# Two-layer decoder trunk in fp32: norm gains folded into weights, pauses in background weight splitting, and earlier gate weights in layer 0

## The chip, the cores and the metric

The kernel runs on one core of one Trainium2 chip. The metric is the device time of one execution in microseconds (us). The engines are PE (TensorE: matmuls and transposes; PEld is its weight load), DVE (VectorE), ACT (ScalarE), POOL (GpSimd) and SP, whose queue issues every DMA of this kernel. Each engine works through its own instructions strictly in order; an instruction whose input is late holds all that stand behind it on that engine.

## The reference

Two layers on 1024 tokens of width 1024. Layer 0 is gated linear attention (GLA) with 4 heads, layer 1 a sparse attention with an indexer and top-k. Each mixer is followed by a residual, a layer norm and a gated embedding.

```python
def layer_norm(x, g, b):
    mu = jnp.mean(x, axis=-1, keepdims=True)
    var = jnp.mean(jnp.square(x - mu), axis=-1, keepdims=True)
    return (x - mu) * lax.rsqrt(var + NORM_EPS) * g + b

# GLA, after the chunked attention has given o per head (512 wide):
    o = o * lax.rsqrt(jnp.mean(o * o, axis=-1, keepdims=True) + NORM_EPS)
    o = o.reshape(B, L, D_INNER) * gn_g
    return (o * jax.nn.silu(z)) @ w_out

# every layer:
    x = layer_norm(ALPHA * x + y, ln_g[i], ln_b[i])          # ALPHA = 4 ** 0.25
    x = x + (p[i] @ ple_w[i]) * jax.nn.sigmoid(x @ ple_gate_w[i])
```

## The kernel before

Every fp32 product is made of three matmuls: each operand is split into a high part (rounded, by ACT) and a low part (the rest, a subtraction by DVE), and hi x hi, hi x lo and lo x hi are summed. All tiles are 128 x 512 or so.

Layer 0 works on two halves of 512 tokens. In each half it runs over the 4 heads. For a head it computes v, the gate, q and k (`v_phase`, `g_phase`, `qk_phase`); then four chunks of 128 tokens run through the steps s1 to s4 of `core_steps`, spread between the matmuls of the output projection of the head before (`out_phase`) and of z for the next head (`z_phase`). The first head of a half has only z to run beside, so its four chunks are packed into about half the time of the others.

The order of the instructions is written by a recorder, `Flow`. It keeps a clock (`fl.now`) that advances with each recorded matmul, and a heap of steps with due times. The order on every engine comes from these due times and not from the chip. Two background streams are paced by the same clock:

- `Weights` (`W`) loads the weights of layer 0 (`wst`, 512 KB each) and splits them into `whi` (ACT, L173) and `wlo` (DVE, L175) shortly before use.
- `split_ahead`, driven by `bg3`, does the same for the weights that layer 1 and the index projections need. Each of 130 half tiles is loaded into `pst` (L200), split on ACT into `phi` (L209) and on DVE in place (L213), and both parts are stored to DRAM (`whs` L211, `wls` L215). One step is due every 2.15 us of the recorder's clock, three steps a piece.

In the second half the top-k counts of the index scores (`tkj`, `tki`, L1032 and L1082 to L1085) run on DVE beside this.

Names that matter below:

- `y` is the residual sum of a half, 128 x 4 x 1024. `load_y` loads the tokens' x into it (2048 KB) and scales it by ALPHA on POOL (L1185). The memory serves as staging for x in feature order before (`y<-in_x_T`).
- `wa2f` are the weights of the second gate projection of one head, loaded by `g_load` in three small DMAs (L459) and split into `w` by `g_split` (ACT L464, DVE L385).
- `o` is a chunk's output in PSUM, `ot` its copy by DVE (L700), `junk` the ACT pass that sums its squares (L702), `oT` the transpose on PE, `uf` its product with z (DVE L725), `u` the two split parts of that.
- `z` is silu of the gate path (ACT L597), times `gn`, the gain of the group norm, on POOL (L593).
- `tr`, `kh`, `kl`, `Af`, `Ah`, `Al`, `S`, `R` are a chunk's scores and transposed keys, their split parts, and the running state; `m` and `ta` are k and q times their decays.
- `ix`, `rl` and `sc` are the index scores of the first half: PE, relu on ACT (L1014), sum on DVE (L1008, L1010). `zz` at L976 is the value projection's copy. They run while the second half starts (`start_half(1)`, which loads the next x and the first `wst`).

Of the kernel before, what the change touches and what calls it, by code (L numbers as in the profile page):

```python
# [10 lines left out]
F32 = mybir.dt.float32  # L11
# [5 lines left out]
AF = mybir.ActivationFunctionType  # L17
# [30 lines left out]
class Flow:  # L48


    def __init__(self, nc):
        self.pe = nc.tensor
        self.now, self.n, self.heap, self.pacers = 0.0, 0, [], []
# [18 lines left out]
    def chain(self, *steps):  # L72

        (_, first), rest = steps[0], steps[1:]
        first()
        if rest:
            self.after(rest[0][0], lambda: self.chain((0, rest[0][1]), *rest[1:]))
# [60 lines left out]
class Weights:  # L138

    def __init__(self, nc, pool, seq, dram, after):
        self.nc, self.pool, self.seq, self.dram, self.after = nc, pool, seq, dram, after
        self.nd = self.ns = self.nu = self.part = 0
        self.due = 0.0
        self.staged, self.parts, self.ahead = {}, {}, {}

    def pace(self, now):
        if now >= self.due and self.step():
# [2 lines left out]
    def step(self):  # L152
        n, i = self.ns, self.part
        if n == len(self.seq):
            return False
        whole = n not in self.staged and self.seq[n][0] in self.ahead
        if n >= self.nu + (3 if whole and self.seq[self.nu - 1][0][0] != "do" else 2):
            return False
        if i == 0:
            if not whole:  # L160
                self.loads(n + 1)
            self.parts[n] = tuple(self.pool.tile([128, 1024], F32R, tag=t, name=t, bufs=4) for t in ("whi", "wlo"))
        if whole:
            for part, there in zip(self.parts[n], self.ahead[self.seq[n][0]]):
                self.nc.sync.dma_start(part.bitcast(F32), there)
            self.ns += 1
            self.loads(min(self.ns + 1, self.nu + 3))
            return True
        st = self.staged[n]
        hi, lo = self.parts[n]  # L170
        c = slice((i % 2) * 512, (i % 2) * 512 + 512)
        if i < 2:
            self.nc.scalar.activation(hi[:, c], st[:, c], AF.Copy)  # L173
        else:
            self.nc.vector.tensor_sub(lo[:, c], st[:, c], hi[:, c].bitcast(F32))  # L175
        self.part = (i + 1) % 4
        if i == 3:
            self.staged.pop(n)
            self.ns += 1
            self.after(1.5, lambda: self.loads(self.ns + 2))  # L180
        return True
# [73 lines left out]
def trunk_kernel(ctx, tc, x_tok, x_T, p_T, pos, freq, g_q, g_k, g_v, g_z, g_a, g_a2, g_ba, g_gn, g_o,  # L255
# [98 lines left out]
    kflip = cp.tile([128, 8], F32, name="kflip")  # L354
    pool.iota(kflip, pattern=[[128, 8]], base=-254, channel_multiplier=1, allow_small_or_imprecise_dtypes=True)
    ba = cp.tile([128, 8], F32, name="ba")
    gn = cp.tile([128, 16], F32, name="gn")
    lngb = cp.tile([128, 2, 2, 8], F32, name="lngb")
    fq = cp.tile([128, 4], F32, name="fq")
    Afs = []  # L360
# [96 lines left out]
    def g_load(h):  # L457
        for i in range(3):
            nc.sync.dma_start(wa2f[32 * i:32 * i + 16, :], g_a2[:, h * 256:(h + 1) * 256])  # L459
# [127 lines left out]
    def z_phase(u, X):  # L587
        h = u["h"]
        zt = lp.tile([128, 4, HT], F32, tag="z", name="z", bufs=2)
        for b in range(4):  # L590
            def ev(ps, b=b):
                def scale():
                    pool.tensor_scalar(zt[:, b], zt[:, b], gn[:, 4 * h + b:4 * h + b + 1], 0.0,  # L593
                                       op0=OP.mult, op1=OP.add)
                    if b == 3:
                        u["z"] = zt
                chain((0, lambda: act.activation(zt[:, b], ps, AF.Silu)), (0.8, scale))  # L597

            yield from fm_block(("z", 4 * h + b), X, ev)

    def core_steps(u):
# [107 lines left out]
        def s4(c):  # L709
            def f():  # L710
                cs = slice(c * 128, c * 128 + 128)
                fl.req(("o", c) in st, "z" in u, h == 0 or u["prev"].get("out", 0) > c)
                ot = st.pop(("o", c))
                ps = pp.tile([128, 4, 128], F32, tag="oT", name="oT")
                for b in range(4):
                    fl.transpose(ps[:, b], ot[:, b * 128:b * 128 + 128], ident)
                uf = lp.tile([128, 4, 128], F32, tag="uf", name="uf", bufs=2)
                uh, ul = t2k("u", F32R), t2k("u", F32R)

                def done():  # L720
                    rc = slice(c, c + 1)
                    pool.tensor_scalar(u["rs"][:, rc], u["ss"][:, rc], 1.0 / 512.0, EPS, op0=OP.mult, op1=OP.add)
                    pool.tensor_tensor(u["rs"][:, rc], u["rs"][:, rc], mhalf[:, rc], op=OP.pow)
                    u["u"][c] = uh, ul
                chain((0, lambda: dve.tensor_mul(uf, ps, u["z"][:, :, cs])),  # L725
                      (0.8, lambda: split(uh, ul, uf.rearrange("p b t -> p (b t)"), done)))
            return f
# [50 lines left out]
            P.append((ph, pl))  # L778
        return P

    def norm_steps(y, np_):

        st8 = np_.tile([128, 4, 2, 6], F32, tag="bn", name="bn")
        mv = np_.tile([128, 4, 2], F32, tag="mv", name="mv")
        rstd = np_.tile([128, 4], F32, tag="rstd", name="rstd")
        f_done = [False] * 4

        def norm(t):
            def power():
                pool.tensor_scalar(rstd[:, t:t + 1], mv[:, t, 1:2], EPS, 1.0, op0=OP.add, op1=OP.mult)  # L790
                pool.tensor_tensor(rstd[:, t:t + 1], rstd[:, t:t + 1], mhalf[:, :1], op=OP.pow)

            def stats():
                for c in range(2):
                    dve.bn_stats(st8[:, t, c], y[:, t, c * 512:c * 512 + 512])  # L795
                dve.bn_aggr(mv[:, t], st8[:, t])
                power()

            def apply():
                dve.tensor_scalar(y[:, t], y[:, t], mv[:, t, 0:1], rstd[:, t:t + 1],  # L800
                                  op0=OP.subtract, op1=OP.mult)
                f_done[t] = True
            chain((0, stats), (2.0, apply))
        return norm, f_done
# [365 lines left out]
    for half in range(NH):  # L1170
# [9 lines left out]
        y = X.y  # L1180

        def load_y(y=y, half=half):
            nc.sync.dma_start(y, x_tok[half * HT:(half + 1) * HT, :].rearrange("(t p) d -> p t d", p=128))
            for t in range(4):
                pool.tensor_scalar(y[:, t], y[:, t], ALPHA, 0.0, op0=OP.mult, op1=OP.add)  # L1185

        if half == 0:
            for T in range(2):
# [1 line left out]
        for h, u in enumerate(units):  # L1190
            if h == 0:
                fl.run(v_phase(u, X))
                for _ in feeder:
                    pass
                ready = a_phase(X, u.pop("wah"))
                if half == 0:
                    bg.set(rope_tables(), 1.7)

                def first_z():
                    zp = z_phase(u, X)  # L1200
                    for i, _ in enumerate(zp):
                        if i == 6:
                            fl.need(lambda: ready)
                            g_phase(u, ready[0])
                        yield
                fl.run(first_z(), qk_phase(u, X))
                load_y()
                if half == 0:
                    bg.finish()
                    bg3.set(W.split_ahead(later, lp), 2.15)  # L1210
            else:
                fl.need(lambda: "w2" in u)
                g_phase(u, ready[0])
                fl.run(v_phase(u, X), qk_phase(u, X))
            bulk, n = [], 0
            if h:
                bulk.append(out_phase(units[h - 1], y))
                n += 4
            if h < GH - 1:
                g_load(h + 1)  # L1220
                after(8.0, lambda u=units[h + 1]: g_split(u))
                bulk.append(z_phase(units[h + 1], X))
                n += 4
            u["prev"] = units[h - 1]
            steps = core_steps(u)
            spread(steps, fl.now, n * B + 15.5)
            fl.run(*bulk)
            if h == GH - 1:
                Pt = load_p(0, half, lambda: t2k("ah", F32R, 4))
            else:  # L1230
                fl.need(lambda: u.get("late"))
        norm, y_done = norm_steps(y, lp)
        fl.run(out_phase(units[-1], y, norm))
        if half:
            bg.finish()
# [17 lines left out]
        if half == 0:  # L1253
# [15 lines left out]
            rt = lambda: lp.tile([128, HT], F32, tag="ot", name="rl", bufs=2)  # L1269
            steps = [f for T in (2, 3) for f in index_steps(T, scs[T - 2], res, kih, kil, ipsum, rt)]  # L1270
            spread(steps, fl.now + 1.5, 2 * B + 4.5)
            nxt = start_half(1)
            next(nxt[2])

# [331 lines left out]
    for half in range(NH):  # L1606
# [11 lines left out]
        for h, units in enumerate(plan, -1):  # L1618
# [31 lines left out]
            if 0 <= h < 4:  # L1650
                residual(st, y, half, (2 * h, 2 * h + 1), start + 2.2, start + dur)
            fl.run(*(unit(u) for u in units))
        norm, y_done = norm_steps(y, l1)
        if half == 0:
            X = XT()
            feed_by(feed_x2(X, 1), fl.now + 14.0, 2.8)
# [80 lines left out]
```

## Time and profile before

| what | value |
|---|---|
| median of 3 runs | 2029.93 us (2024.05 to 2030.09) |
| the profiled execution | 2029.53 us, span 2027.8 us |
| granted TensorE clock, mean | 0.991 |
| busy in the span: PE, DVE, ACT, POOL | 1969.5, 1488.6, 1040.3, 88.9 us |
| mean DMA rate | 229 GB/s |
| splitting ahead (ACT `phi`) | 130 pieces, first at 101.2 us, last at 1029.4 us |

Times in the rows are us from the start of the span. A row of the timeline gives start, duration, engine, line, operation, out<-in, shapes, and in brackets how long the engine stood idle before it and what ended that. A group's row gives the count, total busy us, mean ns, and the idle time with what ended it.

### The profile page before, as it was taken

Reading aid. Unit: us, or ns where it says so; the run is one execution under the profiler, and the core shown is the slowest. Engines: PE = TensorE matmul, PEld = TensorE weight load, DVE = VectorE, ACT = ScalarE, POOL = GpSimd, SP = SyncE. Lnnn points to the kernel's source line nnn. Section 1 sums busy time; section 2 is a strip of 40 time slices with the busy share of each in tenths; the row PEclk is TensorE's granted clock in tenths of the full one; section 3 lists DMA queues with packets and bytes.
Section 4 is the critical chain, followed back from the end, with each engine's and each line's share of the span. In section 5 each row is a group of like instructions: output and inputs, shape, how many; then the busy total and the mean of one; then the engine's idle time right before and its main releaser. Section 6 shows DMA issues by size and latency. Waiting matters only on the chain.

```text
span 2027.8 us, 26796 instructions
## 1 busy us (share of the span) xinstructions
PE 1969.5 (97%) x9016; PEld 1619.3 (80%) x9016; DVE 1488.6 (73%) x3037; ACT 1040.3 (51%) x1943; POOL 88.9 (4%) x151
## 2 busy tenths in 40 slices
PE   8899999999999899999999999999999999999999
PEld 6678888887777788888788787888778888888877
DVE  5676666686676787877867987677796887777863
ACT  5564545546465645455454666666442553434432
POOL 0010101010000101010100000000000000000000
PEclk9999999999999999999999999999999999999999
DMA  4447575757856475656558387877856998888873
GB/s 148 172 148 232 165 218 164 228 177 238 308 185 224 143 221 176 211 172 217 187 182 285 128 303 269 298 265 255 298 199 219 345 340 295 285 299 280 294 252 146
DMA packets 173946, 464.96 MB, mean 229 GB/s; under 512 B 20080, under 2 KB 20848, under 8 KB 167664
## 3 DMA queue, kind: packets, MB, share of 16 engines
q1 hardware_dynamic: 173808, 463.25, 68.0%
q8 instruction: 71, 1.16, 0.2%
q14 instruction: 67, 0.55, 0.1%
HBM read 331.18 MB, written 131.99 MB: 228 GB/s over the span
## 4 chain that ended last, share of the span: by engine, by line
PE 75%; DVE 10%; DMA 6%; ACT 5%; issue 2%; SPq 1%; POOL 0%; POOLq 0%; ACTq 0%; DVEq 0%
PE pb L58 55%; PE o L58 7%; PE U L58 6%; PE S L58 6%; DMA pst<-in_d_z 1%; DVE wlo L175 1%; DVE bn L795 1%; DMA wls<-pst 1%; DMA sqd<-sq 1%; DMA y<-in_x_T 1%; PE oT L62 1%; DVE pst L213 1%; DMA xst<-x2s 1%; ACT phi L209 1%; PE tr L58 1%
## 5 line engine op out<-in xcount | busy, mean ns | idle before, releaser
L58 PE MATMUL pb<-x,whi 128*128 128x512 f32 x2272 | 711.7, 395 | 3.7 <-ACT whi L173 2.3
L58 PEld LDWEIGHTS pb<-x,whi 128*128 128x128 f32 x2272 | 418.8, 189 | 85.1 <-ACT whi L173 3.2
L58 PE MATMUL pb<-x,wlo 128*128 128x512 f32 x1136 | 445.1, 392 | 0.5 <-DVE wlo L175 0.4
L58 PE MATMUL pb<-whi,u 128*128 128x512 f32 x1024 | 347.9, 400 | 6.0 <-ACT u L393 3.1
L58 PEld LDWEIGHTS pb<-x,wlo 128*128 128x128 f32 x1136 | 214.4, 189 | 48.4 <-DVE wlo L175 2.6
L175 DVE TENSOR_TENSOR wlo<-wst,whi 128x512 fp32r<-128x512 f32 x296 | 198.5, 687 | 62.4 <-ACT whi L173 62.2
L58 PEld LDWEIGHTS pb<-whi,u 128*128 128x128 f32 x1024 | 195.2, 191 | 48.8 <-ACT u L393 3.7
L173 ACT ACTIVATE whi<-wst 128x512 fp32r<-128x512 f32 x296 | 175.0, 622 | 75.6 <-DMA wst<-in_g_o 16.4
L58 PE MATMUL pb<-wlo,u 128*128 128x512 f32 x512 | 202.7, 396 | 0.0
L209 ACT ACTIVATE phi<-pst 128x512 fp32r<-128x512 f32 x130 | 81.5, 627 | 134.4 <-DMA pst<-in_d_z 29.2
L1424 ACT ACTIVATE sq<-P,mx 128x128 f32<-128x128 f32 (+7 forms) x128 | 99.0, 774 | 84.5 <-DVE mx L1417 57.5
L1470 ACT ACTIVATE ph<-PT 128x512 fp32r<-128x512 f32 (+1 forms) x160 | 93.7, 601 | 65.5 <-PE o L58 49.8
L58 PE MATMUL S<-kT,q 128*128 128x512 f32 (+2 forms) x576 | 121.8, 343 | 0.0
L1468 DVE TENSOR_TENSOR PT<-PT,ph 128x512 fp32r<-128x512 f32 (+1 forms) x160 | 101.6, 649 | 20.8 <-ACT ph L1470 20.8
L58 PEld LDWEIGHTS S<-kT,q 128*128 128x128 f32 x576 | 100.7, 188 | 17.7 <-DVE mx L1417 0.7
L58 PEld LDWEIGHTS pb<-wlo,u 128*128 128x128 f32 x512 | 97.8, 191 | 18.8
L213 DVE TENSOR_TENSOR pst<-pst,phi 128x512 fp32r<-128x512 f32 x130 | 89.8, 691 | 19.9 <-ACT phi L209 19.6
L1076 ACT ACTIVATE tk<-sc,tki 128x768 f16<-128x768 f32 (+2 forms) x90 | 92.9, 1033 | 22.4 <-DVE tki L1085 15.8
L58 PE MATMUL o<-ph,vT 128*128 128x512 f32 (+2 forms) x384 | 102.4, 351 | 0.0
L58 PE MATMUL pb<-whi,x 128*128 128x512 f32 x256 | 90.0, 411 | 10.6 <-ACT whi L173 6.2
L1430 DVE STREAM_TRANSPOSE sq<-sq 128x128 f32<-128x128 f32 (+7 forms) x128 | 97.7, 768 | 3.7 <-ACT sq L1424 3.1
L702 ACT ACTIVATE junk<-o 128x512 bf16<-128x512 f32 x32 | 19.1, 597 | 128.1 <-DVE ot L700 128.1
(311 smaller groups left out, 3335.0 us busy)
## 6 DMA issues: line engine op xcount, KB each, us to landing
whi<-whs SPq DMA_DIRECT2D x130, 512.0 KB
wlo<-wls SPq DMA_DIRECT2D x130, 512.0 KB
sqd<-sq SPq DMA_DIRECT2D x192, 256.0 KB
PT<-sqd SPq DMA_DIRECT2D x48, 1024.0 KB
whs<-phi SPq DMA_DIRECT2D x130, 256.0 KB
wls<-pst SPq DMA_DIRECT2D x130, 256.0 KB
wst<-in_g_v SPq DMA_DIRECT2D x32, 512.0 KB
wst<-in_g_z SPq DMA_DIRECT2D x32, 512.0 KB
```

The costliest lines, as they stand in the source:

```text
L58: self.pe.matmul(out, lhsT, rhs, start=start, stop=stop)
L62: self.pe.transpose(out, in_, ident)
L173: self.nc.scalar.activation(hi[:, c], st[:, c], AF.Copy)
L175: self.nc.vector.tensor_sub(lo[:, c], st[:, c], hi[:, c].bitcast(F32))
L209: self.nc.scalar.activation(hi, st.bitcast(F32), AF.Copy)
L213: self.nc.vector.tensor_sub(st, st.bitcast(F32), hi.bitcast(F32))
L795: dve.bn_stats(st8[:, t, c], y[:, t, c * 512:c * 512 + 512])
L1076: act.activation(junk()[:, :n], scs[j], AF.Sign, bias=cand[:, j:j + 1].bitcast(F32), accum_out=cnt[:, j:j + 1])
L1424: act.activation(to, rows, AF.Exp, scale=-1.0, bias=mx, accum_out=sm[:, t:t + 1])
L1430: dve.transpose(x, x)
L1468: dve.tensor_sub(lo, lo.bitcast(F32), hi.bitcast(F32))
L1470: chain((0, lambda: act.activation(hi, lo.bitcast(F32), AF.Copy)), (0.8, second))
```

## The change

Five edits, all in layer 0.

1. The gain `gn` is no longer multiplied into z. It is multiplied into the rows of the output weights `o` while these are split: ACT copies with a gain per partition as its scale, and DVE computes (weight x gain) - high in one instruction instead of weight - high.
2. y is no longer scaled by ALPHA. The mixer's share is divided by ALPHA instead, in the constants of the group norm (`rs`), and the layer norm's epsilon is divided by ALPHA squared (`norm_steps` takes it as an argument now; layer 1 passes the old value).
3. In the first head of a half the gate weights of the second head (`g_load(1)`) are loaded before y and not after it.
4. Splitting ahead pauses: the next step is due no sooner than 9 us after `load_y`, and 14 us after the second half's start is recorded.
5. One step of splitting ahead is due every 2.1 us and no longer every 2.15.

```diff
@@ Weights.step @@
+        key = self.seq[n][0]
+        gain = None
+        if key[0] == "o":
+            row = 4 * key[1] + 2 * key[3] + i % 2
+            gain = self.gains[:, row:row + 1]
         if i < 2:
-            self.nc.scalar.activation(hi[:, c], st[:, c], AF.Copy)
+            self.nc.scalar.activation(hi[:, c], st[:, c], AF.Copy, scale=1.0 if gain is None else gain)
+        elif gain is None:
+            self.nc.vector.tensor_sub(lo[:, c], st[:, c], hi[:, c].bitcast(F32))
         else:
-            self.nc.vector.tensor_sub(lo[:, c], st[:, c], hi[:, c].bitcast(F32))
+            self.nc.vector.scalar_tensor_tensor(lo[:, c], st[:, c], gain, hi[:, c].bitcast(F32),
+                                                op0=OP.mult, op1=OP.subtract)
@@ z_phase @@
-                def scale():
-                    pool.tensor_scalar(zt[:, b], zt[:, b], gn[:, 4 * h + b:4 * h + b + 1], 0.0,
-                                       op0=OP.mult, op1=OP.add)
-                    if b == 3:
-                        u["z"] = zt
-                chain((0, lambda: act.activation(zt[:, b], ps, AF.Silu)), (0.8, scale))
+                act.activation(zt[:, b], ps, AF.Silu)
+                if b == 3:
+                    u["z"] = zt
@@ core_steps, s4 @@
-                    pool.tensor_scalar(u["rs"][:, rc], u["ss"][:, rc], 1.0 / 512.0, EPS, op0=OP.mult, op1=OP.add)
+                    pool.tensor_scalar(u["rs"][:, rc], u["ss"][:, rc], ALPHA ** 2 / 512.0, ALPHA ** 2 * EPS,
+                                       op0=OP.mult, op1=OP.add)
@@ load_y and its call @@
             nc.sync.dma_start(y, x_tok[half * HT:(half + 1) * HT, :].rearrange("(t p) d -> p t d", p=128))
-            for t in range(4):
-                pool.tensor_scalar(y[:, t], y[:, t], ALPHA, 0.0, op0=OP.mult, op1=OP.add)
+            bg3.due = max(bg3.due, fl.now + 9.0)
...
                 fl.run(first_z(), qk_phase(u, X))
+                g_load(1)
                 load_y()
                 if half == 0:
                     bg.finish()
-                    bg3.set(W.split_ahead(later, lp), 2.15)
+                    bg3.set(W.split_ahead(later, lp), 2.1)
...
             if h < GH - 1:
-                g_load(h + 1)
+                if h:
+                    g_load(h + 1)
...
-        norm, y_done = norm_steps(y, lp)
+        norm, y_done = norm_steps(y, lp, EPS / ALPHA ** 2)
@@ start of the second half @@
             spread(steps, fl.now + 1.5, 2 * B + 4.5)
+            bg3.due = max(bg3.due, fl.now + 14.0)
             nxt = start_half(1)
```

The order of PE's instructions is the same before and after. On the other engines the steps of splitting ahead stand at other places. The line numbers are those of each kernel's own code.

The DMA queue of SP around the first load of y. Before:

```order
L189 DMA wst<-in_g_z 128x1024 x2
L1183 DMA y<-in_x_tok 128x4x1024
L459 DMA wa2f<-in_g_a 16x256 x3
L200 DMA pst<-in_d_ki 128x512
L189 DMA wst<-in_g_v 128x1024
L211 DMA whs<-phi 128x512
```

After:

```order
L199 DMA wst<-in_g_z 128x1024 x2
L469 DMA wa2f<-in_g_a 16x256 x3
L1192 DMA y<-in_x_tok 128x4x1024
L199 DMA wst<-in_g_v 128x1024
L210 DMA pst<-in_d_ki 128x512
L199 DMA wst<-in_g_v 128x1024
L221 DMA whs<-phi 128x512
```

The gate weights moved ahead of y, and the first `pst` load behind the first `wst` load. The second load of y has the gate weights ahead of it in the same way.

DVE at the same place, up to the copy of the first chunk's output. Before:

```order
L385 TENSOR_TENSOR Al<-Af_91,Ah 128x128
L683 COPY R_97<-U 128x512 x2
L213 TENSOR_TENSOR pst<-pst,phi 128x512
L700 COPY ot<-o 128x512
L651 COPY_PREDICATED Af_93<-cmask,tr 128x128
```

After:

```order
L395 TENSOR_TENSOR Al<-Af_91,Ah 128x128
L690 COPY R_97<-U 128x512 x2
L707 COPY ot<-o 128x512
L658 COPY_PREDICATED Af_93<-cmask,tr 128x128
L395 TENSOR_TENSOR w_799<-wa2f,w_799 64x256
```

The subtraction of splitting ahead no longer stands ahead of the copy.

ACT in the first head of the second half, between the sums of squares (`junk`) of the third and the fourth chunk. Before:

```order
L702 ACTIVATE junk,ss<-o 128x512
L620 ACTIVATE S<-R_97,mid 128x512
L659 ACTIVATE Ah<-Af_93 128x128
L620 ACTIVATE S<-R_97,mid 128x512
L597 ACTIVATE z<-pb 128x512
L173 ACTIVATE whi<-wst 128x512
L209 ACTIVATE phi<-pst 128x512
L393 ACTIVATE u<-uf 128x512
L173 ACTIVATE whi<-wst 128x512
L702 ACTIVATE junk,ss<-o 128x512
```

After:

```order
L709 ACTIVATE junk,ss<-o 128x512
L219 ACTIVATE phi<-pst 128x512
L627 ACTIVATE S<-R_97,mid 128x512
L666 ACTIVATE Ah<-Af_93 128x128
L627 ACTIVATE S<-R_97,mid 128x512
L602 ACTIVATE z<-pb 128x512
L180 ACTIVATE whi<-wst 128x512
L403 ACTIVATE u<-uf 128x512
L180 ACTIVATE whi<-wst 128x512
L219 ACTIVATE phi<-pst 128x512
L709 ACTIVATE junk,ss<-o 128x512
```

`phi` moved from ahead of `u` to behind it, and the piece before it moved to just behind the third `junk`.

ACT at the start of the second half, from the first `wst` split to the first relu of the index scores. Before:

```order
L946 ACTIVATE u<-zz 64x512 x2
L940 ACTIVATE zz<-pb 128x512
L173 ACTIVATE whi<-wst 128x512
L209 ACTIVATE phi<-pst 128x512
L173 ACTIVATE whi<-wst 128x512
L1014 ACTIVATE rl<-ix 128x384 x3
```

After:

```order
L219 ACTIVATE phi<-pst 128x512
L954 ACTIVATE u<-zz 64x512 x2
L948 ACTIVATE zz<-pb 128x512
L180 ACTIVATE whi<-wst 128x512 x2
L1022 ACTIVATE rl<-ix 128x384 x3
```

`phi` is gone from between the two pieces; the two that stood further on, ahead of `zz` at L976, are behind it now.

More of the change, by code (lines that the diff above doesn't have):

```diff
@@ L146, in __init__ @@
         self.staged, self.parts, self.ahead = {}, {}, {}
+        self.gains = None
     def pace(self, now):
@@ L356, in trunk_kernel @@
     ba = cp.tile([128, 8], F32, name="ba")
-    gn = cp.tile([128, 16], F32, name="gn")
+    gn = W.gains = cp.tile([128, 16], F32, name="gn")
     lngb = cp.tile([128, 2, 2, 8], F32, name="lngb")
@@ L779, in load_p, with norm_steps @@
         return P
-    def norm_steps(y, np_):
+    def norm_steps(y, np_, eps):
         st8 = np_.tile([128, 4, 2, 6], F32, tag="bn", name="bn")
@@ L789, in power @@
             def power():
-                pool.tensor_scalar(rstd[:, t:t + 1], mv[:, t, 1:2], EPS, 1.0, op0=OP.add, op1=OP.mult)
+                pool.tensor_scalar(rstd[:, t:t + 1], mv[:, t, 1:2], eps, 1.0, op0=OP.add, op1=OP.mult)
                 pool.tensor_tensor(rstd[:, t:t + 1], rstd[:, t:t + 1], mhalf[:, :1], op=OP.pow)
@@ L1652, in trunk_kernel @@
             fl.run(*(unit(u) for u in units))
-        norm, y_done = norm_steps(y, l1)
+        norm, y_done = norm_steps(y, l1, EPS)
         if half == 0:
```

## The prediction

> **What bounds the kernel now.** I read the page's busy times and the chain that ended last, then layer 0 in stretches of 25 us, then what ended each PE gap there.
>
> ```profile
> PE 1969.5 (97%) x9016; PEld 1619.3 (80%) x9016; DVE 1488.6 (73%) x3037; ACT 1040.3 (51%) x1943; POOL 88.9 (4%) x151
> ...
> PE 75%; DVE 10%; DMA 6%; ACT 5%; issue 2%; SPq 1%; POOL 0%; POOLq 0%; ACTq 0%; DVEq 0%
> ```
>
> PE is busy 97% of the span and carries 75% of the chain. Work on other engines is worth time only where PE waits for it. POOL, from which the change takes most, is 0% of the chain.
>
> In the windows below the columns are the stretch, its length, the busy time of PE, PEld, DVE, ACT and POOL, the granted clock, the DMA share and GB/s.
>
> ```profile
> 350.00:375.00 25.00, 25.00 (x112) 20.73 (x111) 16.27 (x34) 18.59 (x30) 0.00 (x0) 1.00 0.57 187
> ...
> 1030.00:1055.00 25.00, 25.00 (x112) 20.69 (x111) 15.00 (x24) 12.04 (x21) 0.00 (x0) 1.00 0.47 147
> ```
>
> Most of layer 0 looks like these two: PE is full, and DVE and ACT have 6 to 13 us to spare. The change can gain only where that is not so, and the trace has three such places. A is the first attention head of the first half, just after the 2 MB load of y.
>
> ```profile
> 89.09 0.43 SPq L1183 DMA_DIRECT2D y<-in_x_tok  x1
> 89.57 1.85 SPq L459 DMA_DIRECT2D wa2f<-in_g_a  x3
> 91.46 0.85 SPq L200 DMA_DIRECT2D pst<-in_d_ki  x1
> 94.30 0.35 SPq L189 DMA_DIRECT2D wst<-in_g_v  x1
> 100.58 4.51 POOL L1185 TENSOR_SCALAR y<-y 128x1024 f32<-128x1024 f32 x4 [29.74 <-DMA y<-in_x_tok]
> 101.25 0.63 ACT L209 ACTIVATE phi<-pst 128x512 fp32r<-128x512 f32 x1 [7.92 <-DMA pst<-in_d_ki]
> 101.91 1.26 DVE L213 TENSOR_TENSOR pst<-pst,phi 128x512 fp32r<-128x512 f32 x1 [6.24 <-ACT phi L209]
> 103.83 1.05 PE L62 MATMUL oT<-ident,ot 128*128 128x128 f32 x4 [4.02 <-DVE ot L700]
> 106.66 0.63 ACT L173 ACTIVATE whi<-wst 128x512 fp32r<-128x512 f32 x1
> ...
> 104.00:108.00 4.00, 4.00 (x14) 3.28 (x14) 1.18 (x3) 4.00 (x11) 2.52 (x5) 0.58 0.28 108
> ```
>
> Read it from the bottom of the queues up. The first piece of splitting ahead (pst) is issued at 91.46, behind y, and lands at 101.25, right after y at 100.58. ACT stands 7.92 us at its split, DVE 6.24 us at the subtraction behind it, and the copy of ot, which needs neither, queues behind that. PE waits 4.02 us, and then runs 4 us at a granted clock of 0.58, which is another 4.00 x 0.42 = 1.68.
>
> C is the same head in the second half.
>
> ```profile
> 645.00 0.49 PE L58 MATMUL tr<-ta,m 128*128 128x128 f32 x2 [1.92 <-DVE m L579]
> 646.43 1.56 SPq L459 DMA_DIRECT2D wa2f<-in_g_a  x3
> 657.98 0.42 ACT L464 ACTIVATE w<-wa2f 128x256 fp32r<-128x256 f32 x1 [3.30 <-DMA wa2f<-in_g_a]
> 658.42 0.57 DVE L385 TENSOR_TENSOR w<-wa2f,w 64x256 fp32r<-64x256 f32 x1 [4.83 <-ACT w L464]
> 660.04 0.58 PE L58 MATMUL U<-v,kl 128*128 128x512 f32 x1 [2.45 <-DVE kl L385]
> 679.46 0.66 PE L62 MATMUL oT<-ident,ot 128*128 128x128 f32 x4 [0.77 <-DVE ot L700]
> 685.47 0.63 ACT L209 ACTIVATE phi<-pst 128x512 fp32r<-128x512 f32 x1 [2.79 <-DMA pst<-in_d_q]
> 686.66 0.69 DVE L385 TENSOR_TENSOR u<-uf,u 128x512 fp32r<-128x512 f32 x1 [2.54 <-ACT u L393]
> 689.88 0.66 PE L62 MATMUL oT<-ident,ot 128*128 128x128 f32 x4 [2.91 <-DVE ot L700]
> ...
> 660.10:664.00 3.90, 3.90 (x10) 3.06 (x11) 2.96 (x4) 2.36 (x6) 3.25 (x5) 0.56 0.43 159
> 690.00:695.00 5.00, 5.00 (x17) 3.71 (x18) 3.02 (x9) 4.25 (x8) 1.43 (x3) 0.66 0.56 206
> ```
>
> Two chains end in PE gaps. The gate weights wa2f, three small loads behind y, land 11 us after issue and hold ACT, DVE and kl. Later a phi that waits 2.79 for its load stands ahead of u on ACT, u holds DVE, DVE holds ot. Each gap is followed by a slow stretch: 3.90 x 0.44 = 1.72 and 5.00 x 0.34 = 1.70.
>
> B is the start of the second half, between the two.
>
> ```profile
> 547.03 0.63 ACT L173 ACTIVATE whi<-wst 128x512 fp32r<-128x512 f32 x1 [4.50 <-DMA wst<-in_g_v]
> 547.56 0.61 ACT L209 ACTIVATE phi<-pst 128x512 fp32r<-128x512 f32 x1
> 548.08 0.61 ACT L173 ACTIVATE whi<-wst 128x512 fp32r<-128x512 f32 x1
> 549.12 1.01 PE L58 MATMUL ix<-v,u 128*128 128x384 f32 x2 [3.65 <-ACT rl L1014]
> 561.36 0.69 DVE L213 TENSOR_TENSOR pst<-pst,phi 128x512 fp32r<-128x512 f32 x1
> 567.98 1.01 PE L62 MATMUL U<-ident,zz 128*128 128x128 f32 x4 [2.80 <-ACT zz L976]
> ...
> 549.12:556.00 6.88, 6.88 (x21) 5.94 (x22) 6.10 (x11) 4.17 (x9) 0.00 (x0) 0.61 0.97 371
> 560.00:568.00 8.00, 4.21 (x16) 2.42 (x15) 7.89 (x14) 6.21 (x13) 0.00 (x0) 1.00 0.47 150
> 568.00:572.00 4.00, 4.00 (x13) 3.34 (x14) 3.86 (x8) 3.97 (x8) 0.00 (x0) 0.57 0.99 311
> ```
>
> Here the first gap is made by a weight load (wst), the second by DVE and ACT, full with 7.89 and 6.21 of 8.00.
>
> **The change, part by part.** Durations of the operations concerned, by form (busy us, mean ns):
>
> ```profile
> L175 DVE TENSOR_TENSOR wlo<-wst,whi 128x512 fp32r<-128x512 f32 x296 | 198.5, 687 | 62.4 <-ACT whi L173 62.2
> L173 ACT ACTIVATE whi<-wst 128x512 fp32r<-128x512 f32 x296 | 175.0, 622 | 75.6 <-DMA wst<-in_g_o 16.4 <-PE pb L58 14.0 <-DMA wst<-in_g_q 13.6
> L624 DVE SCALAR_TENSOR_TENSOR S<-R,mid,S 128x512 fp32r<-128x512 f32 x56 | 42.3, 760 | 1.2 <-ACT S L620 1.1
> L620 ACT ACTIVATE S<-R,mid 128x512 fp32r<-128x512 f32 x56 | 39.2, 714 | 0.0
> L593 POOL TENSOR_SCALAR z<-z,gn 128x512 f32<-128x512 f32 x32 | 24.2, 756 | 390.1 <-ACT z L597 390.1
> ...
> L209 ACT ACTIVATE phi<-pst x130: 614/631/636, 101.2 to 1029.4; 128x512 fp32r<-128x512 f32 x130
> ```
>
> Folded factors. POOL loses the 32 scalings of z (24.2 us) and the 8 of y (4.51 us in the first half, as much in the second). No PE gap of layer 0 ends on POOL, so I take 0. What it gives DVE is bounded by the pst row of A: 1.26 beside POOL's y against 0.69 at 561.36, 0.57 us, inside the 4.02 already counted. The price is on the output weights: 32 tiles (4 heads x 4 x 2 halves), each with two ACT pieces that now read a gain from memory, as L620 does, and two DVE pieces in the form of L624: 64 x (714 - 622) = 5.9 us of ACT and 64 x (760 - 687) = 4.7 us of DVE. They run beside stretches like 350 to 375, with 6.4 and 8.7 us spare in 25, at about 0.18 and 0.15 us a tile: 0 on the path, at worst +2 if the last head's eight tiles, which have the least cover, show whole (8 x 0.33 = 2.6). The norms only get other constants: 0.
>
> Gate weights ahead of y. Three DMA issues, 1.85 us on SP, now stand ahead of y, so y starts up to 1.85 later. The wst load behind it was issued at 94.30 although SP was done with pst at 92.31, so that SP slot costs nothing. In C wa2f no longer lies behind 2 MB: the 4.83 of DVE and the 2.45 of PE go, with the 1.72 of slow clock. What is late next there is the phi queue, which the pause clears. C1 = 2.45 + 1.72 = 4.17.
>
> Pause after y (9 us). In A no phi and no pst subtraction stand ahead of ot any more. The work behind is ot's own 0.68 us copy, which ends long before PE is there: the whole gap goes. A = 4.02 + 1.68 = 5.70. In C the fourth chunk now has u ahead of phi on ACT and no subtraction ahead of ot. Its gap should shrink to that of the chunk before, 0.77, which has DVE's ordinary queue in it: C2 = 2.91 - 0.77 + 1.70 = 3.84. The 1.92 before tr stays: one subtraction still stands ahead of m.
>
> Pause at the start of the second half (14 us). B loses three phi on ACT and two subtractions on DVE ahead of zz. The first gap loses the phi between the two pieces of whi, 548.08 - 547.56 = 0.52; the load that makes the rest of it stays. The second gap is DVE's, which is full: 2 x 0.60 (0.69 less overlap) = 1.2. Bounds 0.5 and all of it, 3.65 + 2.80 + 6.88 x 0.39 + 4 x 0.43 = 10.9; I take B = 1.7, since both rows that end the gaps stay.
>
> Faster pace of splitting ahead, 2.10 instead of 2.15: 130 pieces of three steps and two steps ahead, 392 x 0.05 = 19.6 us earlier, against 9 + 14 + 9 = 32 of pauses: the last piece comes some 12 us later than 1029.4, still before the layer's gate blocks end (PE is full there in 1030 to 1055 and DVE has 10 us spare). Two pieces more there: 0. The 390 steps also fall between other instructions than before; taken as 0, from -1 to +4.6 for one new gap like C's last (2.91 + 1.70).
>
> Sum: 5.70 + 4.17 + 3.84 + 1.7 = 15.4 us. The profiled execution took 2029.53 (span 2027.80), 0.4 below the median of 2029.93: 2029.5 - 15.4 = 2014.
>
> The slow stretches need not go with their gaps. If those of C came from something else than the 2.45 and 2.91 before them, 1.72 + 1.70 = 3.4 of the sum stays away: 12.0, 2017.5. The rows put them right after those gaps (0.56 and 0.66) and none after the 1.92, so I keep 15.4 and give that case 0.05, inside the forecast's own range. It is what the Trainium skill would have, page "TensorE: Matmul & The Clock Gate", section "Why this matters for your kernels": PE falls back to half clock after gaps above about 3 us. By that rule only A's and B's first gap cost clock; in C this trace does not agree with it.
>
> **Rivals.** First, y's 2 MB now stand right ahead of the first wst load, and ACT may stop at that split instead. It lands after y: 100.58, plus two times 0.67 (101.25 - 100.58 for pst's 256 KB), plus up to 1.85 = 103.8; ACT gets to it at 106.66 - 5.70 = 101.0. That is 2.8 us; the o matmuls need Ah behind it. If all of it reaches PE with a slow stretch, A keeps 5.7 - 4.5, and C1 nothing: 2014.1 + 8.7 = 2023. For it: both loads queue as described. Against: z, S and kh, which PE needs first, stand ahead of that split.
>
> Second, B goes nearly whole, because the relief of DVE keeps both gaps short enough for the clock: 2014.1 - (10.9 - 1.7) = 2005. For it: DVE at 7.89 of 8. Against: the 4.50 wait for wst, which nothing here moves.
>
> Third, the change only moves the waits: the pauses are counted on the recorder's clock, and the same phi comes back 9 us later into the same head with the same load to wait for. Then 2029.5. Against: after y's load has landed phi waits far less, 2.79 in the worst row of C.
>
> Fourth, slower: the new phase puts a phi that waits for its load ahead of u or ot more often in the heads without slack. Each costs 4.6. It ends slower than the bound only past 15.4 + 6.1 = 21.5, so from five new gaps on: 2014.1 + 23 = 2037. Against: in the trace the 24 chunks of the other heads have phi everywhere and no such gap.
>
> **How the numbers follow.** 0.3% (6.1 us) is about what a measurement of this kernel can tell from no change. Forecast 0.62 (alone 2009 to 2020: B from 0.5 up to half of its 10.9, one new gap of 4.6, the slow stretches of C kept), first rival 0.15, second 0.09, third 0.09, fourth 0.05. Faster: 0.62 + 0.09 + half of the first rival, which lies at the bound, and a little of the third: 0.80. Same 0.15, slower 0.05. The range leaves out the third and fourth and the outer half of the second: 2006 to 2024.
>
> **What would show it.** After y no phi on ACT waits 8 us, and the granted clock in the 4 us behind the first oT is 1.00. w<-wa2f in C waits for no DMA. The fourth oT of C waits under 1 us. B's two gaps remain, at about 3.1 and 1 to 2 us. The last phi starts before the gate blocks end. Wrong would be a wait of whi for wst in A or C above 2 us with PE behind it, PE waiting in the other heads for u or ot, or splitting still running when layer 1 opens.

## The result and the profile after

The changed kernel takes 2016.59 us (median of 7 runs, 2013.61 to 2020.59), the kernel before, run beside it, 2026.95 (median of 7). The ratio is 0.994, 95% interval 0.9928 to 0.9952. The prediction was 2014, in a range of 2006 to 2024. The profiled execution of after took 2016.59 (span 2014.8) against 2029.53 (span 2027.8), 12.9 less; the medians differ by 10.4, and the ratio is worth 12.2.

The page after, busy times and the shares of the chain that ended last:

```profile
PE 1963.4 (97%) x9016; PEld 1616.3 (80%) x9016; DVE 1487.6 (74%) x3037; ACT 1046.5 (52%) x1943; POOL 53.7 (3%) x111
...
PE 81%; DVE 7%; ACT 5%; DMA 4%; issue 2%; SPq 0%; POOL 0%; POOLq 0%; ACTq 0%; DVEq 0%
```

POOL lost 35 us of work and PE 6 of busy time; the mean granted clock rose from 0.991 to 0.993. The rest that went is waiting: DVE, DMA and SP hold less of the chain.

A after, from the timelines of SP, ACT and PE, and a window in the columns used before (the third number from the right is the granted clock):

```profile
88.33 0.42 SPq L1192 DMA_DIRECT2D y<-in_x_tok  x1
92.46 0.35 SPq L199 DMA_DIRECT2D wst<-in_g_v  x1
92.85 0.47 SPq L210 DMA_DIRECT2D pst<-in_d_ki  x1
101.07 0.62 ACT L219 ACTIVATE phi<-pst 128x512 fp32r<-128x512 f32 x1
97.78 0.60 PE L62 MATMUL oT<-ident,ot 128*128 128x128 f32 x4
...
97.80:101.80 4.00, 4.00 (x21) 3.38 (x20) 3.99 (x8) 2.27 (x5) 0.00 (x0) 1.00 0.13 49
```

The first phi comes behind the first oT and waits for nothing, oT waits for nothing, and the clock behind it is 1.00. No whi waits for a wst that was issued behind y.

C after, in the order of time:

```profile
637.08 0.63 ACT L219 ACTIVATE phi<-pst 128x512 fp32r<-128x512 f32 x1 [3.29 <-DMA pst<-in_d_o]
637.74 0.69 DVE L223 TENSOR_TENSOR pst<-pst,phi 128x512 fp32r<-128x512 f32 x1 [1.81 <-ACT phi L219]
638.35 0.68 DVE L589 TENSOR_TENSOR m<-pb,m 128x512 f32<-128x512 f32 x1
639.09 0.49 PE L58 MATMUL tr<-ta,m 128*128 128x128 f32 x2 [3.21 <-DVE m L589]
650.22 0.41 ACT L474 ACTIVATE w<-wa2f 128x256 fp32r<-128x256 f32 x1
653.08 0.39 PE L58 MATMUL U<-v,kl 128*128 128x512 f32 x1
677.48 0.66 PE L62 MATMUL oT<-ident,ot 128*128 128x128 f32 x4 [0.79 <-DVE ot L707]
...
639.10:644.10 5.00, 5.00 (x17) 4.06 (x18) 4.02 (x9) 2.15 (x5) 0.00 (x0) 0.66 0.83 261
677.60:682.60 5.00, 4.78 (x22) 3.64 (x23) 4.23 (x10) 4.24 (x8) 0.74 (x2) 1.00 0.55 212
```

The two chains of the prediction are gone: w waits for no load, kl holds nothing, and the fourth oT waits 0.79. But tr, ahead of them, waits 3.21 instead of 1.92 and now has a slow stretch (5.00 x 0.34 = 1.70 us lost): a phi stands 3.29 at its load, the subtraction stands behind it, and m, which needs neither, queues behind that.

Another gap is new in the last head of the first half, a place where before had none (DVE, PE, window):

```profile
407.81 0.69 DVE L223 TENSOR_TENSOR pst<-pst,phi 128x512 fp32r<-128x512 f32 x1 [1.84 <-ACT phi L219]
411.34 0.50 PE L58 MATMUL o<-v,Al 128*128 128x512 f32 x1 [2.05 <-DVE Al L395]
...
411.30:415.00 3.70, 3.66 (x11) 2.96 (x12) 3.43 (x6) 0.00 (x0) 0.00 (x0) 0.57 0.26 70
```

Here too DVE stands at a subtraction of splitting ahead, and u, S, wlo, a sum into y and Al queue behind it. But this phi waits for no load: ACT comes to it only at 407.15, behind its own work in this head.

B after (ACT, PE). Both gaps are there, and the last phi of splitting ahead starts when it did:

```profile
542.08 1.15 ACT L180 ACTIVATE whi<-wst 128x512 fp32r<-128x512 f32 x2 [4.27 <-DMA wst<-in_g_v]
543.66 0.62 PE L58 MATMUL ix<-v,u 128*128 128x384 f32 x2 [2.51 <-ACT rl L1022]
561.54 0.75 PE L62 MATMUL U<-ident,zz 128*128 128x128 f32 x4 [2.81 <-ACT zz L984]
...
1029.57 0.62 ACT L219 ACTIVATE phi<-pst 128x512 fp32r<-128x512 f32 x1
```

PE's instructions stand in the same order in both kernels, so the start of one and the same instruction in both profiles gives the balance up to there. Four pairs, before and then after:

```profile
92.66 0.50 PE L58 MATMUL U<-v,kh 128*128 128x512 f32 x1 [0.55 <-ACT kh L653]
135.37 0.50 PE L58 MATMUL pb<-whi,x 128*128 128x512 f32 x1 [1.10 <-ACT z L597]
475.12 0.39 PE L58 MATMUL pb<-u,wlo 128*128 128x512 f32 x1
571.69 0.39 PE L58 MATMUL pb<-wlo,x 128*128 128x512 f32 x1
```

```profile
90.83 0.73 PE L58 MATMUL U<-v,kh 128*128 128x512 f32 x2 [0.86 <-ACT kh L660]
126.70 0.50 PE L58 MATMUL pb<-whi,x 128*128 128x512 f32 x1 [0.22 <-ACT z L602]
470.81 0.39 PE L58 MATMUL pb<-u,wlo 128*128 128x512 f32 x1
565.08 0.54 PE L58 MATMUL pb<-wlo,x 128*128 128x512 f32 x1
```

After is early by 1.83 just before A, by 8.67 behind A, by 4.31 ahead of B, by 6.61 behind B, at tr of C by 645.00 - 639.09 = 5.91, at the fourth oT by 689.88 - 677.48 = 12.40, and at the end by 13.0 (the spans). So A gave 6.84, the stretch with Al took 4.36, B gave 2.30, tr's longer wait took 1.29, and C gave 6.5 from there to its fourth oT. The first 1.83 lie ahead of the first step of splitting ahead, and they differ from one execution to the next: the same row starts at 91.01 with the pause after y alone and at 91.09 with the pace of 2.10 alone, and between 90.31 and 93.75 in the 14 profiles of these runs. Without them the balance at the end is 11.2, between the 10.4 of the medians and the 12.2 of the ratio.

### The profile page after: what moved, and what is told of

Its sections match the earlier page's. It is cut to its first block, busy times and chain, and to the rows that moved or that the text cites. A ratio compares the mean times of both kernels' runs of the same rounds, so it can differ in the third digit from the quotient of the medians.

```text
span 2014.8 us, 26716 instructions
## 1 busy us (share of the span) xinstructions
PE 1963.4 (97%) x9016; PEld 1616.3 (80%) x9016; DVE 1487.6 (74%) x3037; ACT 1046.5 (52%) x1943; POOL 53.7 (3%) x111
## 4 chain that ended last, share of the span: by engine, by line
PE 81%; DVE 7%; ACT 5%; DMA 4%; issue 2%; SPq 0%; POOL 0%; POOLq 0%; ACTq 0%; DVEq 0%
PE pb L58 59%; PE o L58 8%; PE U L58 6%; PE S L58 5%; DMA xst<-x2s 1%; DMA wls<-pst 1%; DMA pst<-in_d_o 1%; DVE bn L803 1%; PE oT L62 1%; PE tr L58 1%; DVE wlo L182 1%; DVE sc L1018 1%; ACT whi L180 0%; DMA wst<-in_g_v 0%; DMA wlo<-wls 0%
## 5 line engine op out<-in xcount | busy, mean ns | idle before, releaser
L182 DVE TENSOR_TENSOR wlo<-wst,whi 128x512 fp32r<-128x512 f32 x232 | 154.8, 684 | 56.2 <-ACT whi L180 56.0
L180 ACT ACTIVATE whi<-wst 128x512 fp32r<-128x512 f32 x232 | 136.4, 621 | 47.2 <-DMA wst<-in_g_z 13.7
```

Source lines behind the costliest of these rows:

```text
L180: self.nc.scalar.activation(hi[:, c], st[:, c], AF.Copy, scale=1.0 if gain is None else gain)
```

## Experiments

All ratios are to the kernel before on the same chip; their 95% intervals stand beside them.

**One edit at a time.** First the folds (edits 1 and 2) alone:

```diff
 # before, and only:
+            self.nc.scalar.activation(hi[:, c], st[:, c], AF.Copy, scale=1.0 if gain is None else gain)
...
+    def norm_steps(y, np_, eps):
```

> The kernel before with the folded factors alone (gain into the output weights, ALPHA into the constants). My theory: POOL was on no path that PE waits for, so within 3 us of the kernel before (about 2027): PE still waits some 4 us at the first oT and 2.4 us for kl in the second half. Rival, POOL's work was what held DVE: most of the 12 us, about 2016. Rival, the longer forms of the output weights' split cost time in the last head, where DVE has least to spare: slower by 2 to 5, a wait of PE for Al or ot there.

2028.61 us, ratio 1.0001 (0.9992 to 1.001). Alone, the 33 us taken from POOL and the 6.5 us given to ACT (busy times of this run's page) are worth nothing.

The gate weights ahead of y (edit 3) alone:

```diff
+                g_load(1)
                 load_y()
...
+                if h:
+                    g_load(h + 1)
```

> The kernel before with the gate weights' load ahead of y alone. My theory: only the wait for kl in the first head of the second half goes, 2.45 us and 1.72 of slow clock: 4.2 us faster, about 2023; the first oT in the first half still waits 4 us. Rival, y started later holds what comes behind it: no gain, 2027.

2030.03 us, ratio 1.0009 (1.0 to 1.0017): no gain, as the rival had it. The kl wait went, and this came right behind it (PE, ACT, SP of this run):

```profile
662.47 0.50 PE L58 MATMUL o<-v,Ah 128*128 128x512 f32 x1 [2.60 <-ACT Ah L659]
661.10 0.63 ACT L209 ACTIVATE phi<-pst 128x512 fp32r<-128x512 f32 x1 [6.14 <-DMA pst<-in_d_z]
647.38 0.42 SPq L1183 DMA_DIRECT2D y<-in_x_tok  x1
647.85 0.50 SPq L215 DMA_DIRECT2D wls<-pst  x1
657.74 0.33 SPq L200 DMA_DIRECT2D pst<-in_d_z  x1
```

Now the store wls is issued right behind the 2 MB of y. The next pst load goes into one of only two buffers, and SP stands 7.3 us at it until that store has landed; it is issued 9.9 us after the store. phi waits 6.14 for that load, and Ah stands behind phi. Moving one small load out of the way of y passes the wait to the next that is in its way.

The two pauses (edit 4) alone, at the old pace:

```diff
+            bg3.due = max(bg3.due, fl.now + 9.0)      # in load_y
...
+            bg3.due = max(bg3.due, fl.now + 14.0)     # before start_half(1)
```

> The kernel before with the two pauses alone (pace 2.15). My theory: the first oT's wait goes (5.7 us), the second half's start gains 2, the last oT of the first head of the second half 3.8, the wait for kl (4.2) stays: 7 to 11 us faster, 2016 to 2020, less what the new places of the splitting steps cost elsewhere. Rival, the waits only move: within 3 us of 2027.

2014.7 us, ratio 0.9935 (0.9923 to 0.9948), as large a gain as the whole change's, and 1.3 us below the range expected. The wait for kl did not stay: with wa2f still behind y it is down to

```profile
649.58 0.50 PE L58 MATMUL U<-v,kl 128*128 128x512 f32 x1 [0.62 <-DVE kl L385]
```

against 2.45 before. The change without the folds (edits 3, 4 and 5) belongs here too:

```diff
 # the changed kernel without edits 1 and 2
-                act.activation(zt[:, b], ps, AF.Silu)
+                chain((0, lambda: act.activation(zt[:, b], ps, AF.Silu)), (0.8, scale))
```

> The changed kernel without the folded factors (pauses, gate weights, pace 2.10). My theory: the folds are worth nothing, so 2016 to 2017 as the changed kernel. Rival, the longer forms made the new wait for Al at 411 us: that wait goes and it is 3 to 4 us faster than the changed kernel, about 2013. Rival, the folds carried the gain: 2024 or more.

2017.02 us, ratio 0.9952 (0.994 to 0.9965), as the theory had it. Al waits 1.90 here too, so the new Al gap does not come from the longer split with a gain. But in C two waits came back that after does not have. The order on DVE is the same in both there (POOL, DVE and PE of this run, then DVE and PE of after):

```profile
650.84 5.47 POOL L1186 TENSOR_SCALAR y<-y 128x1024 f32<-128x1024 f32 x4 [27.97 <-DVE kl L385]
652.42 1.53 DVE L624 SCALAR_TENSOR_TENSOR S<-R,mid,S 128x512 fp32r<-128x512 f32 x1
659.84 0.66 PE L62 MATMUL oT<-ident,ot 128*128 128x128 f32 x4 [0.83 <-DVE ot L700]
```

```profile
653.44 0.75 DVE L631 SCALAR_TENSOR_TENSOR S<-R,mid,S 128x512 fp32r<-128x512 f32 x1
660.13 0.60 PE L62 MATMUL oT<-ident,ot 128*128 128x128 f32 x4
```

Beside POOL's scaling of y this S takes DVE 1.53 us instead of 0.75, the next wlo 1.53 instead of 0.68, and the second and third oT wait 0.83 and 0.50. From tr to the fourth oT this run takes 38.61 us; after takes 38.39 with a slow stretch of 1.70 in it, so 36.7 without. So by these two profiles the folds are worth about 1.9 us in C beside the other edits. The whole times do not tell this apart: 0.9952 and 0.994 have intervals that overlap.

**Which pause, and the pace.** The pause after y alone:

```diff
 # before, and only:
+            bg3.due = max(bg3.due, fl.now + 9.0)      # in load_y
```

> The kernel before with the 9 us pause after y alone. Theory (the pause after y clears A and both chains of C): A falls by about 7.5 us, the new wait before o<-v,Al at 411 us comes as in the run of both pauses and takes about 4 back, B stays at 3.65 and 2.80, C gives about 8: 2016 to 2018 us. Rival (the pause at the start of the second half carries a large part): 2021 to 2024, with C's gaps still there.

2019.94 us, ratio 0.9957 (0.9942 to 0.9971), by its median 2 above the end of what was expected. It clears A's oT (a wait of 1.43 for kl comes behind it) and the kl chain, but not C's last gap, which the prediction had given to it:

```profile
679.09 0.66 PE L62 MATMUL oT<-ident,ot 128*128 128x128 f32 x4 [2.94 <-DVE ot L700]
```

With the pause at the second half's start the ratio is 0.9935, but the two intervals overlap, so what that pause adds is not settled.

The kernel before at the pace of 2.10 alone (edit 5):

```diff
-                    bg3.set(W.split_ahead(later, lp), 2.15)
+                    bg3.set(W.split_ahead(later, lp), 2.1)
```

> The kernel before at the pace of 2.10 instead of 2.15, and nothing else. Theory (a pace only draws new places for the same steps): A as before, other gaps of 2 to 4 us come and go, 2023 to 2033 us. Rival (a faster pace is a gain or loss of its own): splitting ends about 20 us earlier, under 2022 or over 2034.

2020.73 us, ratio 0.9969 (0.9955 to 0.9984): by the number the rival's, a gain of 6. The first oT of A still waits 3.46. The oT of the row above, without any pause:

```profile
683.16 0.65 PE L62 MATMUL oT<-ident,ot 128*128 128x128 f32 x4 [0.78 <-DVE ot L700]
```

And the changed kernel at 2.15:

```diff
-                    bg3.set(W.split_ahead(later, lp), 2.1)
+                    bg3.set(W.split_ahead(later, lp), 2.15)
```

> The changed kernel at the old pace of 2.15. Theory (folds and gate weights are worth nothing, the pace only sets the phase): the same as both pauses alone, 2014 to 2015.5 us, with the first gap of B at about 0.8 us and Al near 2.0. Rival (the pace of 2.10 is a gain of its own, since splitting ends earlier): 2018 or more, with the loss at the end of layer 0.

2010.58 us, ratio 0.9911 (0.9897 to 0.9925), 4 better than expected. Against both pauses alone only the gate weights and the folds are added, which were taken for nothing. But tr of C starts 0.81 us earlier than there (635.51 and 636.32) and the fourth oT 3.86 earlier (672.41 and 676.27), both with a clock of 1.00 in between: of the 4.0 us between the two profiles 3.05 lie between these two rows, and by the run above about 1.9 of them belong to the folds. The intervals of the two ratios (0.9935 and 0.9911) just overlap.

So the pace of 2.10 gains 0.3% without the other edits and loses 0.3% with them (0.994 against 0.9911, by intervals that just fail to touch; those of a later measurement of after, 0.9935, do overlap). A gain of the rate itself, as the rival had it, would have the same sign in both; what counts is where the steps come to stand.

**The two new gaps.** The changed kernel with two of its 130 subtractions moved on DVE, by three instructions and by one, and nothing else on any engine (the number in `hold` is the step's; the first time of its pair is the earliest on the recorder's clock at which it may be recorded, the second is when the step after it is due, as it was):

```diff
-        if self.gen is not None and now >= self.due:
+        if self.gen is not None and now >= self.due and now >= self.hold.get(self.n, (0.0, 0.0))[0]:
...
+bg3.hold = {135: (361.5, 362.498), 222: (558.3, 560.195)}
```

> The changed kernel with two of its 130 DVE subtractions of splitting ahead moved by three and by one instruction: behind u, S and wlo ahead of the Al of 411 us, and behind the m of 638 us. Nothing else moves on any engine. Theory (these two subtractions, which wait for phi, make the two new gaps and their slow stretches): Al waits under 0.5 us instead of 2.05, tr under 0.5 instead of 3.2, the clock behind both is 1.00, and the time falls by about 7 us to 2008 to 2011. Rival (the work is only put off, and the next wait takes it): 2014 to 2017, with a new gap at the Af or kl behind them.

2016.56 us, ratio 0.9937 (0.9922 to 0.9952), in 6 runs from 2011.12 to 2018.9: the time expected, 2008 to 2011, was missed, and it is not told apart from after's. Its profile (an execution of 2013.38; PE, and a window where Al's gap was):

```profile
543.29 1.01 PE L58 MATMUL ix<-v,u 128*128 128x384 f32 x2 [4.09 <-ACT rl L1022]
634.74 0.49 PE L58 MATMUL tr<-ta,m 128*128 128x128 f32 x2 [1.02 <-DVE m L589]
...
409.50:413.50 4.00, 3.98 (x20) 3.40 (x21) 4.00 (x7) 0.10 (x1) 0.00 (x0) 1.00 0.60 180
```

Al's gap and its slow stretch are gone, and so its subtraction did make this gap. tr waits 1.02 with no slow stretch, less than in either profile of after (3.21, and 1.80 without a slow stretch in the second one below), but not under 0.5. And PE now comes to B earlier and waits there 4.09 instead of 2.51.

**B's first gap.** The prediction said of the 4.50 us wait for wst "which nothing here moves". What moves it stands on SP (after; then the run with the one store moved, with its ACT and PE):

```profile
535.15 0.32 SPq L221 DMA_DIRECT2D whs<-phi  x1
536.49 0.42 SPq L199 DMA_DIRECT2D wst<-in_g_v  x1
```

```profile
533.41 0.49 SPq L199 DMA_DIRECT2D wst<-in_g_v  x1
535.84 0.63 ACT L219 ACTIVATE phi<-pst 128x512 fp32r<-128x512 f32 x1 [1.14 <-DMA pst<-in_d_q]
539.83 1.15 ACT L180 ACTIVATE whi<-wst 128x512 fp32r<-128x512 f32 x2 [0.18 <-DMA wst<-in_g_v]
545.91 0.62 PE L58 MATMUL ix<-v,u 128*128 128x384 f32 x2 [2.13 <-DVE u L955]
```

In after SP stands 4.2 us at whs until phi, itself late for its load, is done, and the loads of x and wst stand behind. In before SP stood in the same place 2.5 us at whs and 2.4 at the pst load behind it, which waited for a wls store, and wst was issued at 540.94. The edit:

```diff
+bg3.hold = {189: (480.0, 480.0), 190: (0.0, 492.995)}
```

> The changed kernel with one store of splitting ahead (whs), the pst load and the subtraction that belong to it moved from ahead of the second half's first loads (x and wst) to behind them; phi and the rest stay, and the next wls and phi move by one or two instructions. Theory (the first gap of B is SP's: its queue stands at this whs until phi is done, and the wst loads stand behind it): wst is issued about 3 us earlier, whi waits 1 to 2 us for it instead of 4.27, the ix wait falls from 2.5 to about 0.8, and 3 us go. Rival (the 4.27 is the transfer itself, as the prediction had it): the ix wait stays at 2.5 or more and the time does too.

2013.21 us, ratio 0.9923 (0.9908 to 0.9938). Although phi is later here than in after, wst is issued 3 us earlier, whi waits 0.18, and no ix waits over 0.8 for rl: the wait for wst is SP's, as the theory had it, and not the transfer's. But 2.13 comes back at another ix, which waits for u on DVE, so in the time the rival is half right, and it is not told apart from after's.

All three moves together:

```diff
+bg3.hold = {135: (361.5, 362.498), 189: (480.0, 480.0), 190: (0.0, 492.995), 222: (558.3, 560.195)}
```

> The changed kernel with this store and both subtractions (Al, tr) moved. Theory (the three losses add up): 4 from the subtractions, by the profile of the run with two moved, and 3 to 4 from the store: 7 to 8 us under the changed kernel on the same chip. Rival (the waits only pass to the next place): under 4 us.

2010.57 us, ratio 0.9904 (0.9889 to 0.9919), beside after once more on the same chip:

> The changed kernel once more, beside the three on the same chip: 0.993 to 0.995 of the kernel before, with the waits of 2.05 (Al), 2.5 (ix), 2.8 (zz) and 3.2 (tr) as in the first profile, if these belong to the order of the instructions. Rival (they belong to the single run): one of them differs by over 1 us.

2015.94 us, ratio 0.9935 (0.9919 to 0.9951). Three steps in other places are worth 5.4 us by the medians. That is between the two expectations, and the two intervals just touch. The waits of the second profile of after:

```profile
410.84 0.57 PE L58 MATMUL o<-v,Al 128*128 128x512 f32 x1 [2.05 <-DVE Al L395]
543.66 0.62 PE L58 MATMUL ix<-v,u 128*128 128x384 f32 x2 [3.33 <-ACT rl L1022]
637.49 0.49 PE L58 MATMUL tr<-ta,m 128*128 128x128 f32 x2 [1.80 <-DVE m L589]
```

Al and zz (2.80) repeat to 0.01 us: they are made by the order on an engine, as the theory had it. ix (3.33 against 2.51) and tr (1.80 against 3.21) end in a load's arrival and move by about a microsecond from run to run, tr by 1.41, which is the rival's case.

**A faster version.** The changed kernel at 2.15 with the two subtractions of its own Al and tr moved:

```diff
-                    bg3.set(W.split_ahead(later, lp), 2.1)
+                    bg3.set(W.split_ahead(later, lp), 2.15); bg3.hold = {132: (361.5, 362.598), 216: (558.3, 559.077)}
```

> The changed kernel at the pace of 2.15 with its two subtractions at the same places moved (Al, and tr behind m). Theory: at 2.15 the whs store already stands behind the loads, Al's gap goes (2), tr's 2.65 halves (DVE is full there, m still stands behind other work), so 3 to 4 us under the same kernel without the moves, 9 or more under the changed kernel, about 0.9895 of the kernel before. Rival: no better than 2.15 alone, 0.991.

2008.23 us, ratio 0.9892 (0.9876 to 0.9909), 7.7 under after on the same chip, by intervals that do not touch (9 or more was expected). Al's gap is gone, and tr waits 1.96. Against the same kernel without the moves (0.9911) it is not settled.

## Why the prediction was right, and where it was not

The time came out 2.6 us above the forecast and well inside the range, and some of its steps are shown. A's wait and slow stretch went with the pause after y (5.70 said, 6.84 between the rows around A, which hold another 0.88 at a wait for z). The rival that ACT stops at the first wst behind y did not come: no whi of A waits for a wst issued behind y, and phi and oT wait for nothing. The slower rival's phi that waits for its load came once, at tr, and stood ahead of m there; at Al the phi was late on ACT and not at its load.

The folds were taken as 0. Alone they are (ratio 1.0001). Beside the pauses they are worth about 1.9 us in C by one pair of profiles, which the prediction missed: it bounded what POOL's work costs DVE by A's one row, and did not look at the scaling of y in C.

C gave more than the sum had (the 2.45 is gone, the 2.91 is down to 0.79 with a clock of 1.00 behind it, and the 0.44 and 0.77 of the second and third oT of before are gone too), but for other reasons than its steps gave. C1 was put down to the gate weights: alone they bring nothing (2.60 at Ah in place of 2.45 at kl), and the pauses alone take kl down to 0.62. C2 was put down to the pause: with the pause after y alone that oT waits 2.94, and with a faster pace and no pause it waits 0.78. What frees it is where phi falls, and either edit can bring that about.

The step that was mis-sized is the last one, "The 390 steps also fall between other instructions than before; taken as 0". It bounded the loss at one new gap of 4.6. There were two losses: a new gap at Al (4.36 between the rows around it, 2.05 + 1.71 of them Al's own) and a longer one at tr (1.29 more wait and 1.70 of slow clock). Its lower bound of -1 was also too near: in the kernel before the new pace alone is worth 0.31%, 6 us. That these 7.35 us of loss make so small a miss is luck, because other terms went the other way: 1.83 at the start, which vary between executions, and 3.62 more than said in the three places (A 1.14, B 0.6, C 6.49 + 1.70 + 1.70 against 8.01). 15.4 + 1.83 + 3.62 - 7.35 is 13.5, and 0.5 of it is lost again up to the end.

B was 2.30 where 1.7 was said, but its steps are not as said. Its first gap fell to 2.51 where 3.1 was said, and to 3.33 in the second profile. The reason given for it, a load that nothing moves, was wrong: the load's issue waits on SP's queue behind a store. Its second gap was to shrink to 1 to 2 with two subtractions less on DVE, and did not: zz waits 2.80 or 2.81 in all 14 profiles, with a subtraction of splitting ahead among the sums of the index scores before it (561.36 in before) or with none (after). So splitting ahead does not make this gap; ACT and DVE work there in turn on relu and sum of the last scores, and ACT comes to zz only then. No run here moves it.

The last phi came at 1029.57 and not 12 us later than 1029.4: the delay of 12 on the recorder's clock and the 12 to 13 us that the layer became shorter cancel.

## What to carry to other kernels

Background work that is interleaved by a clock has a phase, and a change of its pace or a pause redraws all places after it. Give that redraw a term with a range of its own (here 6 us either way on 2028, as large as the largest single term of the sum), and time a change at two or three paces before it is credited to an edit. When a load seems slow, look first at what its issuing queue stands at: a store that waits for a late producer holds every load behind it. An edit that takes one victim out of a queue should be tested alone, since the next victim may be 2 us behind it. An edit that is worth nothing alone should be timed again beside the others, as the folds show.

## What the runs showed of the hardware

A gap's length alone does not decide whether PE's clock falls. The wait for zz is 2.80 or 2.81 us in all 14 profiles. Behind it the clock falls in 13 of them, and in the run with the two subtractions moved it does not (that run; then after):

```profile
561.03 0.66 PE L62 MATMUL U<-ident,zz 128*128 128x128 f32 x4 [2.80 <-ACT zz L984]
...
561.00:565.00 4.00, 3.97 (x20) 3.35 (x21) 3.86 (x8) 3.97 (x8) 0.00 (x0) 1.00 0.69 265
```

```profile
561.50:565.50 4.00, 3.96 (x13) 3.27 (x14) 3.86 (x8) 3.97 (x8) 0.00 (x0) 0.57 0.68 261
```

Al waits 1.96 with both pauses and with the pause after y alone; the clock falls behind the first and not behind the second. The shortest wait here behind which it fell is 1.90 (Al without the folds).

How long it stays down differs too. Behind the 2.45 of before, slices of 1 us from 660.10 on were granted 0.60, 0.50, 0.50 and 0.69 and then 1.00: the shares below 1 add up to 1.71, that is 3.42 us at one half. Of the 35 falls behind waits of over 1 us in the 14 profiles (80 to 1100 us) 24 cost 1.70 or 1.71 us and four less (1.39 to 1.65). The other seven cost 2.5 to 3.1, behind waits of 2.80 to 4.09, so a gap's price is not one number.

The Trainium skill, page "TensorE: Matmul & The Clock Gate", section "What's actually happening", says that the clock is judged in windows of 3413 ns that run freely, without regard to the kernel. The 3.42 of most falls agrees, and a free window could let one wait of 2.80 pass and catch another; that this is the reason is argued from the lengths and not shown by a run.
